# The small matmuls of the attention and of y between the big matmuls of the next slot, not in blocks between slots

## The chip, the cores and the metric

One NeuronCore of a Trainium2 chip runs the whole kernel. The metric is the time of one execution on the device, in microseconds (us). The engines are named PE (TensorE, matmuls), PEld (its weight loads), DVE (VectorE), ACT (ScalarE), POOL (GpSimd) and SP (SyncE, which issues DMAs).

## The reference: what is computed

One layer of a decoder trunk on x of 512 x 2048, float32. All of it is written with matmuls whose float32 operands are split exactly into a high and a low part (hi, lo), so that one product takes three matmuls.

```python
h = x @ w_in + b_in            # q,k,v,z of three branches, forget logits, three merge gates
o_fox  = fox_attention(...)    # 8 heads, causal, bias from cumulative log-sigmoid of the forget logits
o_swa  = swa_attention(...)    # 8 q heads / 2 kv heads, window 128, sinks, ALiBi
o_moba = moba_attention(...)   # 8 heads, blocks of 256, top-3 past blocks and the own one, ALiBi
br_i = (merge_heads(o_i) * silu(z_i)) @ w_branch_i
y = sum_i sigmoid(gate_i) * br_i
out = layer_norm(2 ** 0.25 * x + y @ w_out)
```

## The kernel before

The program is unrolled by Python; tiles carry their dependencies, and each engine runs its instructions in the order in which they are written. First come the V projection and the merge gates (up to about 530 us), which the change leaves alone. Then the main loop (line 1040) runs over a stream of weight tiles `ids`, one tile of 128x512 per **slot**: "h" slots (four per projected tile of 128 columns, `proj_step`), "v" slots (the V of moba, `mv_step`, 16 of them), "b" slots (branch products, four per group of 512 columns and branch, `branch_step`) and "o" slots (output product, `out_step`). An h, b or o slot issues 12 matmuls of 512 columns, a v slot 24 of 256 columns. These are the big matmuls.

At each slot i the loop first issues the high part of the weights of slot i + 2 on ACT (`prepare`), then the slot's big matmuls, then the tasks that were put down for slot i, sorted by an order number. The low part of those weights (`lower`, on DVE) is a task of order 2; when it is done it lets SP load raw weights further ahead. Three buffers hold the split weights.

The attention is put down as tasks by `plan_pair`. A head has four units (one for each 128 queries). A unit that begins at slot s does: scores at s, order 8 (`unit_scores`, two matmuls of 128 to 512 columns); maximum on DVE at s + 1, order 0 (`unit_max`) and exponential on ACT, order 5; reciprocal on DVE and scaling on POOL at s + 2, order 1; transposes at s + 3, order 8 (`unit_turn`, one to four of 128x128); their high part on ACT and low part on DVE at s + 4, orders 1 and 6. A head's values (`head_values`, 8 matmuls of 128 to 512 columns) are at order 8 six slots after its last unit began; its low half on ACT and its sum on DVE come one slot later, orders 2 and 7. Units begin 1.5 slots apart (fox, three pairs of heads of moba) or 1 slot apart (swa, the last pair). Order 8 comes last in a slot, so these matmuls stand in a block between the big matmuls of two slots. Projected tiles are evacuated one and two slots after their end, at orders 2 and 3 (`q_upper`, `k_lower` and so on).

In the b slots a group's fourth slot is followed by `branch_evac` (order 9: four products with the gates on DVE, and for two of three branches four sums). After the third branch of a block of 512 columns, `turn_y` runs at order 8 two and three slots later, twice each: four transposes and a split of the result, high part on ACT, low part on DVE.

PSUM has two sets of tiles: "acc" with three (projections, one of a branch's four, transposes of y) and "att" with five (scores, transposes, values, three of a branch's four).

Of the kernel before, what the change touches and what calls it, by code (L numbers as in the profile page):

```python
# [13 lines left out]
P = 128  # L14
# [73 lines left out]
def hybrid_kernel(ctx: ExitStack, tc: tile.TileContext, a: dict, out: bass.AP):  # L88
    nc = tc.nc
# [9 lines left out]
    ident = stage.tile([P, P], F32, name="ident", bufs=1)  # L99
# [9 lines left out]
    def acc_tile(name):  # L109
        return psum.tile([P, S], F32, tag="acc", name=name, bufs=3)  # L110

    def att_tile(name):
        return psum.tile([P, S], F32, tag="att", name=name, bufs=5)

    def split(raw, hi, lo):
        nc.scalar.activation(hi, raw, AF.Copy)  # L116
        nc.vector.tensor_sub(lo, raw, hi.bitcast(F32))  # L117
# [7 lines left out]
    def at(i, order, f, *args):  # L125
        tasks.setdefault(i, []).append((order, len(tasks.get(i, ())), f, args))
# [6 lines left out]
    def prepare(i):  # L133

        if i >= len(ids) or i in parts:
            return None
        load(i // 2)
        raw = raws[i // 2][:, (i % 2) * S:(i % 2 + 1) * S]
        if i in held:
            hi, lo = held[i]  # L140
        else:
            hi = stage.tile([P, S], F32R, tag="hi", name="hi")
            lo = stage.tile([P, S], F32R, tag="lo", name="lo")
        parts[i] = (hi, lo)
        nc.scalar.activation(hi, raw, AF.Copy)  # L145

        def lower():
            nc.vector.tensor_sub(lo, raw, hi.bitcast(F32))  # L148
            for d in range(1, raw_bufs):
                load(i // 2 + d)  # L150

        return lower
# [324 lines left out]
    for n in range(items):  # L477
        sc, m = divmod(n, 56)
# [85 lines left out]
        nc.sync.dma_start(a["scratch"], rows[:NH])  # L564


    halves = (slice(0, HD), slice(HD, P))

    def q_upper(acc, t, res):
# [56 lines left out]
    def unit_scores(kind, h, i, env, u):  # L626
        if i == 0:
            env["pth"] = work.tile([P, 13, P], F32R, tag="pth", name="pth")
            env["ptl"] = work.tile([P, 13, P], F32R, tag="ptl", name="ptl")
        u["k0"] = max(i - 1, 0) if kind == "swa" else 0  # L630
        u["n"] = (i + 1 - u["k0"]) * P
        ks = slice(u["k0"] * P, (i + 1) * P)
        qs, (kh, kl) = env["q"][env["e"]], env["k"][env["g"]]
        qi = qs[:, i * P:(i + 1) * P]
        s = u["s"] = att_tile("s")[:, :u["n"]]
        nc.tensor.matmul(s, qi, kh[:, ks], start=True, stop=False)
        nc.tensor.matmul(s, qi, kl[:, ks], start=False, stop=True)

    def unit_max(kind, h, i, env, u):
        n = u["n"]  # L640
# [32 lines left out]
        nc.gpsimd.tensor_scalar(lt, lt, st[:, 3:4], 1.0, op0=ALU.mult, op1=ALU.mult)  # L673

    def unit_turn(kind, h, i, env, u):
        pt = u["pt"] = att_tile("pt").rearrange("p (b c) -> p b c", c=P)
        for b in range(u["n"] // P):
            nc.tensor.transpose(pt[:, b], u["lt"][:, b * P:(b + 1) * P], ident)

    def cells(kind, i, u):  # L680
        nb = u["n"] // P
# [7 lines left out]
        nc.vector.tensor_sub(env["ptl"][:, c], u["pt"][:, :u["n"] // P], env["pth"][:, c].bitcast(F32))  # L689

    def head_values(kind, h, env):
        o = env["o"] = att_tile("o")
        for kb in range(4):
            q1 = min(kb + 2, 4) if kind == "swa" else 4
            cell = 2 * kb if kind == "swa" else 4 * kb
            for m, pp in enumerate((env["pth"], env["ptl"])):
                nc.tensor.matmul(o[:, kb * P:q1 * P], env["v"]()[:, kb, env["vh"]], pp[:, cell:cell + q1 - kb],
                                 start=(kb == 0 and m == 0), stop=(kb == 3 and m == 1), skip_group_check=True)

    def head_low(kind, h, env):  # L700
        mine = halves[env["e"]]
# [48 lines left out]
    def proj_step(i):  # L750
        _, t, c = ids[i]
        if c == 0:
            accs[t] = acc_tile(f"h{t}")
        hi, lo = parts.pop(i)
        for j in range(4):
            k, cc = 4 * c + j, slice(j * P, (j + 1) * P)
            nc.tensor.matmul(accs[t], hi[:, cc], xh[:, k], start=(k == 0), stop=False)  # L757
            nc.tensor.matmul(accs[t], hi[:, cc], xl[:, k], start=False, stop=False)  # L758
            nc.tensor.matmul(accs[t], lo[:, cc], xh[:, k], start=False, stop=(k == KD - 1))  # L759
        if c == 3:  # L760
            for d, order, f, res in ends[t]:
                at(i + d, order, f, accs[t], t, res)
# [3 lines left out]
    def mv_step(i):  # L766
        _, hf, g = ids[i]
        if g == 0:
            mv_acc[hf] = [acc_tile(f"mv{hf}{j}") for j in range(2)]
        hi, lo = parts.pop(i)  # L770
        for j in range(2):
            k, cc = 2 * g + j, slice(j * 256, (j + 1) * 256)
            for st in range(4):
                o = mv_acc[hf][st // 2][:, (st % 2) * 256:(st % 2 + 1) * 256]
                lx = slice(st * P, (st + 1) * P)
                nc.tensor.matmul(o, xh[:, k, lx], hi[:, cc], start=(k == 0 and st % 2 == 0), stop=False,
                                 skip_group_check=True)
                nc.tensor.matmul(o, xl[:, k, lx], hi[:, cc], start=False, stop=False, skip_group_check=True)
                nc.tensor.matmul(o, xh[:, k, lx], lo[:, cc], start=False, stop=(k == KD - 1),
                                 skip_group_check=True)  # L780
        if g == 6:
            mv_acc["b", hf] = work.tile([P, S], F32, tag="T", name="vbm")[:, :256]
            nc.sync.dma_start(mv_acc["b", hf], a["bm"][hf:hf + 1].to_broadcast([P, 256]))
        if g == 7:
            for st in range(4):
                at(i + st // 2, 9, mv_evac, hf, st)
# [22 lines left out]
    t = 0  # L809
    last_att = 0  # L810
    for p in range(4):
        q, k, z = [], [], []
# [28 lines left out]
    for p in range(4):  # L841
        q, k, z = [], [], []
# [12 lines left out]
    sigs, ys = {}, {}  # L855
# [18 lines left out]
    def branch_step(i):  # L874
        _, g, kt = ids[i]
        b = g % 3
        if kt == 0:
            for st in range(4):
                bracc[g, st] = (acc_tile if st == 3 else att_tile)("br")
        hi, lo = parts.pop(i)  # L880
        oh, ol = box["ozh"], box["ozl"]
        for st in range(4):
            ss = slice(st * P, (st + 1) * P)
            for n, (w, o) in enumerate([(hi, oh), (hi, ol), (lo, oh)]):
                nc.tensor.matmul(bracc[g, st], o[:, 4 * b + kt, ss], w, start=(kt == 0 and n == 0),  # L885
                                 stop=(kt == 3 and n == 2))
        if kt == 3:
            at(i, 9, branch_evac, g)
            if b == 2:
                for dt in range(4):  # L890
                    at(i + 2 + dt // 2, 8, turn_y, g // 3, dt)
# [14 lines left out]
    yb = {}  # L906

    def turn_y(dblk, dt):
        if not yb:
            yb["h"] = keep.tile([P, KD, S], F32R, tag="bigh", name="yh")  # L910
            yb["l"] = keep.tile([P, KD, S], F32R, tag="bigl", name="yl")
        yt = acc_tile("yt")
        for st in range(4):
            nc.tensor.transpose(yt[:, st * P:(st + 1) * P], ys[dblk, st][:, dt * P:(dt + 1) * P], ident)
        k = 4 * dblk + dt
        split(yt, yb["h"][:, k], yb["l"][:, k])

    zr, stats = [], []

# [18 lines left out]
    def out_mm(st, k, hi, lo, half=None):  # L938

        sl = slice(st * P, (st + 1) * P)  # L940
        o = oacc[st]
        if half is not None:
            cs = slice(half * 256, (half + 1) * 256)
            o, hi, lo = oacc[3 + half][:, :256], hi[:, cs], lo[:, cs]
        nc.tensor.matmul(o, yb["h"][:, k, sl], hi, start=(k == 0), stop=False)  # L945
        nc.tensor.matmul(o, yb["l"][:, k, sl], hi, start=False, stop=False)  # L946
        nc.tensor.matmul(o, yb["h"][:, k, sl], lo, start=False, stop=(k == KD - 1))  # L947
# [6 lines left out]
    def out_step(i):  # L954
        _, ec, k = ids[i]
        if k == 0:
            for st in range(4):
                oacc[st] = (acc_tile if st == 3 else att_tile)("o")
            if ec == 3:
                oacc[4] = acc_tile("o")  # L960
        if ec == 3 and k >= 4:
            return
        hi, lo = parts.pop(i)
        for st in range(3 if ec == 3 else 4):
            out_mm(st, k, hi, lo)
        if ec == 3:
            out_mm(3, k, hi, lo, 0)
            out_mm(3, k, hi, lo, 1)
        if k == KD - 1:
            for st in range(4):  # L970
                at(i, 9, residual, ec, st, oacc[st])
# [68 lines left out]
    for i in range(len(ids)):  # L1040
        assert i in parts
        lower = prepare(i + 2)
        if lower:
            at(i, 2, lower)
        step[ids[i][0]](i)
        for _, _, f, args in sorted(tasks.pop(i, ()), key=lambda x: x[:2]):
            f(*args)
    first = where["o", 3] + 4
# [83 lines left out]
```

## Time and profile before

| | us |
|---|---|
| runs | 1342.1, 1343.46, 1650.02 |
| median of the runs | 1343.46 |
| the profiled execution | 1342.68 |
| its span, which the trace covers | 1341.0 |
| PE busy in the span | 1323.1 |
| DVE / ACT / POOL busy | 906.3 / 647.6 / 177.2 |

The granted clock of PE is at its full level over all but the first and last of the 40 slices of the page. A matmul's row begins when it is taken up and its end is modelled, so rows of matmuls overlap; prices on PE are read from starts, over a stretch that begins and ends among big matmuls.

### The profile page before, as it was taken

How to read it: one execution, taken by the hardware profiler on the slowest of the kernel's cores; microseconds unless marked ns; L12 is line 12 of the kernel's file. 1: busy time of each engine (PE TensorE's matmuls, PEld its weight loads, DVE VectorE, ACT ScalarE, POOL GpSimd, SP SyncE). 2: the span in 40 equal slices, each digit the busy share in tenths (PEclk: the TensorE clock that was granted, in tenths of full speed). 3: DMA queues.
4: the chain of work that ended last, by engine and by line, in shares of the span. 5: the costliest groups of instructions: out<-in, count | busy, mean ns of one | idle time of the engine just before them, and what ended most of it. 6: DMA issues, size and time to landing. Idle time of an engine off the chain costs nothing.

```text
span 1341.0 us, 18413 instructions
## 1 busy us (share of the span) xinstructions
PE 1323.1 (99%) x6435; PEld 1115.8 (83%) x6435; DVE 906.3 (68%) x1629; ACT 647.6 (48%) x1195; POOL 177.2 (13%) x249
## 2 busy tenths in 40 slices
PE   8999999999999999999999999999999999999996
PEld 8888888888888888888889998888888888888885
DVE  7888888888888887566665656555646666532356
ACT  5445645455554645556564556565654222222231
POOL 4700000000000000111222333121220000000005
PEclk9999999999999999999999999999999999999998
DMA  7634427080633514432323232322225555453323
GB/s 246 223 142 163 159 65 266 9 300 29 214 116 112 211 32 145 152 96 80 110 71 99 64 86 77 94 67 92 71 81 183 185 188 189 158 218 94 94 95 126
DMA packets 57804, 174.43 MB, mean 130 GB/s; under 512 B 6552, under 2 KB 8088, under 8 KB 56944
## 3 DMA queue, kind: packets, MB, share of 16 engines
q1 hardware_dynamic: 46672, 145.87, 33.4%
q0 software_dynamic: 2976, 13.48, 2.9%
q10 hardware_dynamic: 8064, 13.91, 2.8%
q8 instruction: 50, 0.82, 0.2%
q14 instruction: 42, 0.34, 0.1%
HBM read 155.12 MB, written 18.12 MB: 129 GB/s over the span
## 4 chain that ended last, share of the span: by engine, by line
PE 97%; DVE 1%; issue 0%; DMA 0%; SPq 0%; ACT 0%; DVEq 0%; ACTq 0%
PE br L885 10%; PE h L757 9%; PE h L759 9%; PE h L758 9%; PE beta L325 5%; PE beta L323 5%; PE beta L324 5%; PE o L947 4%; PE o L945 4%; PE o L946 4%; PE gamma L325 3%; PE alpha L325 3%; PE gamma L323 3%; PE gamma L324 3%; PE alpha L323 3%; PE alpha L324 3%
## 5 line engine op out<-in xcount | busy, mean ns | idle before, releaser
L145 ACT ACTIVATE hi<-raw 128x512 fp32r<-128x512 f32 x248 | 156.3, 631 | 321.9 <-PE o L946 97.5
L148 DVE TENSOR_TENSOR lo<-raw,hi 128x512 fp32r<-128x512 f32 x248 | 174.1, 706 | 153.1 <-ACT hi L145 128.5
L757 PE MATMUL h<-xh,hi 128*128 128x512 f32 x528 | 208.0, 394 | 0.0
L759 PE MATMUL h<-xh,lo 128*128 128x512 f32 x528 | 206.6, 391 | 0.0
L758 PE MATMUL h<-xl,hi 128*128 128x512 f32 x528 | 206.1, 390 | 0.0
L759 PEld LDWEIGHTS h<-xh,lo 128*128 128x128 f32 x528 | 99.1, 188 | 21.8 <-DVE lo L148 0.3
L758 PEld LDWEIGHTS h<-xl,hi 128*128 128x128 f32 x528 | 99.3, 188 | 18.6
L757 PEld LDWEIGHTS h<-xh,hi 128*128 128x128 f32 x528 | 99.2, 188 | 18.5
L673 POOL TENSOR_SCALAR lt<-lt,st 128x128 f32<-128x128 f32 (+2 forms) x96 | 70.7, 737 | 289.5 <-DVE st L672 287.6
L116 ACT ACTIVATE ghi<-rawb 128x512 fp32r<-128x512 f32 x96 | 60.7, 633 | 69.8 <-DVE glo L117 47.3
L116 ACT ACTIVATE ghi<-rawd 128x512 fp32r<-128x512 f32 x96 | 60.7, 633 | 69.8 <-DVE glo L117 52.1
L116 ACT ACTIVATE ghi<-rawa 128x512 fp32r<-128x512 f32 x96 | 60.6, 633 | 52.0 <-PE alpha L324 17.3
L117 DVE TENSOR_TENSOR glo<-rawd,ghi 128x512 fp32r<-128x512 f32 x96 | 66.4, 691 | 24.0 <-ACT ghi L116 21.8
L945 PE MATMUL o<-hi,yh 128*128 128x512 f32 (+1 forms) x212 | 81.8, 386 | 0.0
L946 PE MATMUL o<-hi,yl 128*128 128x512 f32 (+1 forms) x212 | 81.7, 385 | 0.0
L947 PE MATMUL o<-lo,yh 128*128 128x512 f32 (+1 forms) x212 | 81.7, 385 | 0.0
L117 DVE TENSOR_TENSOR glo<-rawb,ghi 128x512 fp32r<-128x512 f32 x96 | 66.3, 690 | 18.8 <-ACT ghi L116 17.7
L325 PE MATMUL alpha<-glo,xh 128*128 128x512 f32 x192 | 75.2, 392 | 0.4 <-DVE glo L117 0.4
L885 PE MATMUL br<-hi,ozh 128*128 128x512 f32 x192 | 75.3, 392 | 0.0
L885 PE MATMUL br<-lo,ozh 128*128 128x512 f32 x192 | 74.9, 390 | 0.0
L325 PE MATMUL beta<-glo,sh 128*128 128x512 f32 x192 | 74.8, 390 | 0.0
L323 PE MATMUL alpha<-ghi,xh 128*128 128x512 f32 x192 | 74.8, 389 | 0.0
(231 smaller groups left out, 3108.5 us busy)
## 6 DMA issues: line engine op xcount, KB each, us to landing
raw<-in_ws SPq DMA_DIRECT2D x130, 512.0 KB, 3.5
rawc<-in_wa SPq DMA_DIRECT2D x24, 512.0 KB, 5.7
rawd<-in_wa SPq DMA_DIRECT2D x24, 512.0 KB, 5.5
sig<-gate_tiles SPq DMA_DIRECT2D x48, 256.0 KB, 3.9
rawb<-in_wa SPq DMA_DIRECT2D x20, 512.0 KB, 3.6
rawa<-in_wa SPq DMA_DIRECT2D x20, 512.0 KB, 4.8
rawv<-in_wv SPq DMA_DIRECT2D x15, 324.0 KB, 4.3
xraw<-in_xT SPq DMA_DIRECT2D x16, 256.0 KB, 4.8
```

The source lines that it names most:

```text
L116: nc.scalar.activation(hi, raw, AF.Copy)
L145: nc.scalar.activation(hi, raw, AF.Copy)
L148: nc.vector.tensor_sub(lo, raw, hi.bitcast(F32))
L323: nc.tensor.matmul(o, sth[:, us], hi, start=first, stop=False, skip_group_check=True)
L324: nc.tensor.matmul(o, stl[:, us], hi, start=False, stop=False, skip_group_check=True)
L325: nc.tensor.matmul(o, sth[:, us], lo, start=False, stop=last, skip_group_check=True)
L757: nc.tensor.matmul(accs[t], hi[:, cc], xh[:, k], start=(k == 0), stop=False)
L758: nc.tensor.matmul(accs[t], hi[:, cc], xl[:, k], start=False, stop=False)
L759: nc.tensor.matmul(accs[t], lo[:, cc], xh[:, k], start=False, stop=(k == KD - 1))
L885: nc.tensor.matmul(bracc[g, st], o[:, 4 * b + kt, ss], w, start=(kt == 0 and n == 0), stop=(kt == 3 and n == 2))
L945: nc.tensor.matmul(o, yb["h"][:, k, sl], hi, start=(k == 0), stop=False)
L946: nc.tensor.matmul(o, yb["l"][:, k, sl], hi, start=False, stop=False)
```

## The change

A list `small` is set up. The score matmuls, the transposes of the attention, the value matmuls, the transposes of y and the split of y behind them are no longer issued at their order in the slot, but put on that list as closures, in the order in which they were issued. In the next slot `begin_small(12)` sets how many closures one `tick()` takes from it (one up to twelve entries, two up to 24), and after each big matmul a `tick()` follows (two after three matmuls in a v slot, three after three in an o slot). What is left after the slot's big matmuls is issued then, ahead of the slot's other tasks. The PSUM tile of a score, transpose or value is taken when its first closure runs. Nothing else moves: the tasks that read the results keep their slots and orders.

```diff
+    small, rate = [], [1]
+
+    def begin_small(n):
+        rate[0] = max(1, -(-len(small) // n))
+
+    def tick(n=None):
+        for _ in range(rate[0] if n is None else n):
+            if small:
+                small.pop(0)()
...
-        s = u["s"] = att_tile("s")[:, :u["n"]]
-        nc.tensor.matmul(s, qi, kh[:, ks], start=True, stop=False)
-        nc.tensor.matmul(s, qi, kl[:, ks], start=False, stop=True)
+
+        def upper():
+            u["s"] = att_tile("s")[:, :u["n"]]
+            nc.tensor.matmul(u["s"], qi, kh[:, ks], start=True, stop=False)
+
+        small.append(upper)
+        small.append(lambda: nc.tensor.matmul(u["s"], qi, kl[:, ks], start=False, stop=True))
...
-        pt = u["pt"] = att_tile("pt").rearrange("p (b c) -> p b c", c=P)
+        def turn(b):
+            if b == 0:
+                u["pt"] = att_tile("pt").rearrange("p (b c) -> p b c", c=P)
+            nc.tensor.transpose(u["pt"][:, b], u["lt"][:, b * P:(b + 1) * P], ident)
+
         for b in range(u["n"] // P):
-            nc.tensor.transpose(pt[:, b], u["lt"][:, b * P:(b + 1) * P], ident)
+            small.append(lambda b=b: turn(b))
...
+        def value(kb, m):
+            if kb == 0 and m == 0:
+                env["o"] = att_tile("o")
             q1 = min(kb + 2, 4) if kind == "swa" else 4
             cell = 2 * kb if kind == "swa" else 4 * kb
...
+        for kb in range(4):
+            for m in range(2):
+                small.append(lambda kb=kb, m=m: value(kb, m))
...
             nc.tensor.matmul(accs[t], hi[:, cc], xh[:, k], start=(k == 0), stop=False)
+            tick()
             nc.tensor.matmul(accs[t], hi[:, cc], xl[:, k], start=False, stop=False)
+            tick()
             nc.tensor.matmul(accs[t], lo[:, cc], xh[:, k], start=False, stop=(k == KD - 1))
+            tick()
...
                 nc.tensor.matmul(o, xh[:, k, lx], lo[:, cc], start=False, stop=(k == KD - 1),
                                  skip_group_check=True)
+                tick()
+                tick()
...
                 nc.tensor.matmul(bracc[g, st], o[:, 4 * b + kt, ss], w, start=(kt == 0 and n == 0),
                                  stop=(kt == 3 and n == 2))
+                tick()
...
-        yt = acc_tile("yt")
+        box_y, k = {}, 4 * dblk + dt
+
+        def turn(st):
+            if st == 0:
+                box_y["t"] = acc_tile("yt")
+            nc.tensor.transpose(box_y["t"][:, st * P:(st + 1) * P], ys[dblk, st][:, dt * P:(dt + 1) * P], ident)
+
         for st in range(4):
-            nc.tensor.transpose(yt[:, st * P:(st + 1) * P], ys[dblk, st][:, dt * P:(dt + 1) * P], ident)
-        k = 4 * dblk + dt
-        split(yt, yb["h"][:, k], yb["l"][:, k])
+            small.append(lambda st=st: turn(st))
+        small.append(lambda: split(box_y["t"], yb["h"][:, k], yb["l"][:, k]))
...
             out_mm(st, k, hi, lo)
+            tick()
+            tick()
+            tick()
...
+        begin_small(12)
         step[ids[i][0]](i)
+        tick(len(small))
```

## Rows read from the trace of the kernel before

**Rows 1.** The page, part 1: engine, busy us (share of the span), instructions.

```profile
PE 1323.1 (99%) x6435; PEld 1115.8 (83%) x6435; DVE 906.3 (68%) x1629; ACT 647.6 (48%) x1195; POOL 177.2 (13%) x249
```

**Rows 2.** Waits of PE, whole span: us in total, times, longest us.

```profile
PE vc L251 <- DVE lo L117: 2.4, 3, 1.5
...
PE gamma L325 <- DVE glo L117: 0.4, 1, 0.4
```

**Rows 3.** Groups by line and form, PE: count, busy us, mean ns.

```profile
L678 PE MATMUL pt<-ident,lt 128*128 128x128 f32 x216 | 39.6, 274 | 0.0
...
L914 PE MATMUL yt<-ident,y 128*128 128x128 f32 x64 | 8.3, 272 | 0.0
...
L636 PE MATMUL s<-kh,qs 128*128 128x128 f32 x24 | 7.2, 299 | 0.0
```

**Rows 4.** Timeline of PE, big matmuls in a row: start us, us.

```profile
676.64 0.39 PE L757 MATMUL h<-xh,hi 128*128 128x512 f32 x1
...
681.18 0.39 PE L759 MATMUL h<-xh,lo 128*128 128x512 f32 x1
```

**Rows 5.** Timeline of PE, eight transposes of y between big matmuls.

```profile
1054.90 0.39 PE L885 MATMUL br<-lo,ozh 128*128 128x512 f32 x1
1055.13 1.03 PE L914 MATMUL yt<-ident,y 128*128 128x128 f32 x8
...
1056.46 0.40 PE L885 MATMUL br<-lo,ozh 128*128 128x512 f32 x1
```

**Rows 6.** Timeline of PE, two transposes alone between big matmuls.

```profile
831.75 0.39 PE L759 MATMUL h<-xh,lo 128*128 128x512 f32 x1
831.98 0.38 PE L678 MATMUL pt<-ident,lt 128*128 128x128 f32 x2
...
832.90 0.40 PE L757 MATMUL h<-xh,hi 128*128 128x512 f32 x1
```

**Rows 7.** Timeline of PE, the running sum's four matmuls between big ones.

```profile
545.77 0.39 PE L759 MATMUL h<-xh,lo 128*128 128x512 f32 x1
545.99 0.74 PE L560 MATMUL csum<-tri,pair 128*128 128x512 f32 x4
...
547.33 0.40 PE L757 MATMUL h<-xh,hi 128*128 128x512 f32 x1
```

**Rows 8.** Timeline of PEld, weight loads around two scores of 128 columns.

```profile
844.34 0.19 PEld L636 LDWEIGHTS s<-kh,qs 128*128 128x128 f32 x1
844.57 0.19 PEld L637 LDWEIGHTS s<-kl,qs 128*128 128x128 f32 x1
844.68 0.19 PEld L757 LDWEIGHTS h<-xh,hi 128*128 128x128 f32 x1
844.79 0.19 PEld L758 LDWEIGHTS h<-xl,hi 128*128 128x128 f32 x1
```

**Rows 9.** Timelines of PE and DVE, a block with values and after it.

```profile
674.03 0.39 PE L697 MATMUL o<-pth,vfox 128*128 128x512 f32 x1
...
675.95 0.40 PE L757 MATMUL h<-xh,hi 128*128 128x512 f32 x1
...
676.33 0.55 DVE L652 CUSTOM_DVE_ANT_0 lt<-s,row 128x384 f32<-128x384 f32 x1
...
677.28 0.67 DVE L148 TENSOR_TENSOR lo<-raw,hi 128x512 fp32r<-128x512 f32 x1
```

**Rows 10.** Tiles yt and br, 1050 to 1066: ns min/median/max of one.

```profile
L116 ACT ACTIVATE yh<-yt x4: 594/596/598, 1055.8 to 1059.9; 128x512 fp32r<-128x512 f32 x4
L117 DVE TENSOR_TENSOR yl<-yt,yh x4: 680/686/692, 1056.4 to 1060.6; 128x512 fp32r<-128x512 f32 x4
...
L899 DVE TENSOR_TENSOR y<-br,sig x4: 679/679/681, 1061.8 to 1063.6; 128x512 f32<-128x512 f32 x4
```

**Rows 11.** Windows, the part with attention: busy us by engine, clock, DMA.

```profile
530.00:1017.00 487.00, 487.00 (x2573) 416.62 (x2572) 281.95 (x721) 279.43 (x577) 109.77 (x169) 1.00 0.30 93
```

More of the change, by code (lines that the diff above doesn't have):

```diff
@@ L691, in head_values @@
     def head_values(kind, h, env):
-        o = env["o"] = att_tile("o")
-        for kb in range(4):
+        pth, ptl = env["pth"], env["ptl"]
+        def value(kb, m):
+            if kb == 0 and m == 0:
+                env["o"] = att_tile("o")
             q1 = min(kb + 2, 4) if kind == "swa" else 4
             cell = 2 * kb if kind == "swa" else 4 * kb
-            for m, pp in enumerate((env["pth"], env["ptl"])):
-                nc.tensor.matmul(o[:, kb * P:q1 * P], env["v"]()[:, kb, env["vh"]], pp[:, cell:cell + q1 - kb],
-                                 start=(kb == 0 and m == 0), stop=(kb == 3 and m == 1), skip_group_check=True)
+            nc.tensor.matmul(env["o"][:, kb * P:q1 * P], env["v"]()[:, kb, env["vh"]],
+                             (pth, ptl)[m][:, cell:cell + q1 - kb], start=(kb == 0 and m == 0),
+                             stop=(kb == 3 and m == 1), skip_group_check=True)
+        for kb in range(4):
+            for m in range(2):
+                small.append(lambda kb=kb, m=m: value(kb, m))
     def head_low(kind, h, env):
```

## The prediction

> **What bounds the kernel now.** I read the page first, then TensorE's waits, then TensorE's order of time where small matmuls stand between big ones, then VectorE's and ScalarE's rows at the two places where the change makes somebody wait. The page gives TensorE 99% of the span [rows 1]. Its waits add up to 6.7 us and all of them are before the attention: its five kinds belong to the V projection, the warm-up and the gates [rows 2] (first and last of the five). So from the projections of the attention on, TensorE never stands still, and what the change can win there is not a wait. It can only be the price that a small matmul has on TensorE.
>
> How many are there? 216 transposes of the attention and 64 of y [rows 3]; 24 heads with 4 units of two score matmuls, 192; 24 heads with 8 value matmuls, 192. In all 664. Today they stand in about 111 blocks: 8 of y, the others one at the end of each slot that has any (counted from the planner's slots).
>
> The prices follow from start times. Twenty big matmuls in a row take 681.18 - 676.64 = 4.54 us, 0.227 each [rows 4]. Eight transposes: from the last big one before them at 1054.90 to the third big one after, 1056.46, are 1.56 us; three big ones are 0.68, so 0.88 is left, 0.110 per transpose [rows 5]. Two transposes alone: 832.90 - 831.75 = 1.15 us with four big ones (0.91) leaves 0.24, so 0.12 each [rows 6]. A block thus costs 0.11 per transpose and 0.02 once, for leaving it. A single 128-column matmul of the other kind is seen once, as the last of the four of the running sum: 547.33 - 545.77 = 1.56 us less four big ones leaves 0.65; its 1,280 columns at 0.227 per 512 are 0.567, so the last one, with 0.057 for its columns, cost 0.057 + 0.083 = 0.14 [rows 7].
>
> Why 0.11 and not 0.057? The weight loads show it. Around a pair of 128-column scores the loads start at 844.34 (under the big one), 844.57, 844.68 and 844.79 [rows 8]. The first small load is hidden by the big matmul. The next two follow 0.11 apart: a load begins when the matmul before it gets going, so only one is ahead, and 128 columns are too short to cover 0.11 of load.
>
> **The change, part by part.** *Removed:* nothing; the same 664 instructions and loads are issued. *Moved on TensorE:* each small one now follows a big one and is followed by a big one (in pairs in the moba V slots, in threes in the output slots). The load of the small one was hidden for the first of a block and is now hidden for all. But the load of the big one behind it has only the small one to hide under, so 0.11 is paid there instead. Per small one I expect no gain, and a bit of the 0.02 on leaving: 664 less 111 blocks, less some 50 that still go in pairs or threes, is 500 new exits. Bounds from the nearest rows: nothing (the 0.02 may lie in how the next few big ones settle, which now overlap), and 0.14 - 0.11 = 0.03 (the single one of the running sum), that is 0 to 15 us. I take half of the 0.02, because transposes are the largest group and the two alone are their nearest row: 500 x 0.01 = 5.0 us. A gain is not excluded by this row alone; it is the first rival.
>
> The Trainium skill, page "TensorE: Matmul & The Clock Gate", section "Back-to-back issue gap", gives about 81 ns per matmul of 128 columns in a stream of loads and matmuls. No such row is here: the trace has 0.11. By the page's figure the 280 transposes would cost 8 us less, an estimate from that page alone.
>
> *Moved for the consumers:* scores, transposes and values, done at a slot's start until now, are done part of the way into it. Lists are mostly of 3 to 6, so they end by mid slot. The worst is a slot with values: 8 values, 2 transposes, 2 scores make 12, one per big one, with the scores last. Such a list costs 675.95 - 674.03 = 1.92 us [rows 9], so the slot lasts 12 x 0.227 + 1.92 = 4.64 us, and the last score ends about 0.4 behind that (a 512-column matmul's row lasts 0.39 [rows 4]). On VectorE the maximum (unit_max) stands ahead of the low half (lower) of the weights for the slot after next. From the maximum's start at 676.33 to the end of the low half behind it at 677.28 + 0.67 are 1.62 us [rows 9]. So these weights are ready 0.4 + 1.62 = 2.0 us into the next slot. They are needed at the third matmul of the slot after: 2.72 + 0.45 = 3.2 us, as the next slot has no list. Spare: about 1.1 us. The exponential behind the maximum on ScalarE delays only the next slot's high half, with a slot to spare. Cost: nothing, hidden by weights prepared two slots ahead; if that cover is gone, it is the second rival. Score and transpose tiles are given back within their own slot, so five suffice. No DMA and nothing on POOL is moved; the loads on SP wait for a low half that is up to 2 us later, and have about three pairs of slots in hand.
>
> *y:* the two transposes-and-splits of a slot now run in the next slot, so the second pair falls into the slot that ends the next branch product, and its splits go ahead of lower and of the evacuation (branch_evac) on VectorE. From that slot's start: nine big and eight transposes, 2.04 + 0.9, then the row of a transpose 0.27 [rows 3], the high part 0.60, the low part 0.69, the first product 0.68 [rows 10] and ahead of it lower with 0.67 [rows 9]: 5.85 us. Of att's five tiles three hold this branch, two are free, so the next branch's third tile waits for that first product. TensorE wants it after 12 big, 8 transposes and 6 big: 4.09 + 0.9 = 5.0 us. That is a new wait of 0.85, three times (the last y falls among the output slots): 2.5 us. Ends: 0 if the tiles are handed out otherwise, and 5 if the split is later by another row.
>
> **Sum**, against the profiled execution's own 1342.68 us (span 1341.0, 1.7 outside; the median of the runs shown, 1343.46, lies 0.8 above): + 5.0 + 2.5 = 1350.2, say 1350. With the bounds alone 1343 to 1363.
>
> **The rivals.** *The loads are hidden after all* (faster). If the chip can have two loads ahead when a big matmul gives it 0.227 for two of 0.11, each 128-column instruction falls from 0.11 to 0.057. These are 280 transposes, 48 scores [rows 3] and 48 values (two per head): 376 x 0.053 = 20 us less, with y's wait + 2.5: 1325. Against it: the running sum's last, with 512, 384 and 256 columns ahead of it, paid 0.14 [rows 7]. For it: only that one is seen. The Trainium skill's page "TensorE: Matmul & The Clock Gate", section "Step-by-step: what each phase is for", says that TensorE's window pulls weight loads ahead of running matmuls into a background buffer; the trace agrees for one load [rows 8], and that page by itself would allow this rival. Chance 0.08.
>
> *Late scores become TensorE's wait* (slower). Place: the third big matmul, two slots after each of the 24 slots with values. It decides once VectorE is over 1.1 us further behind there than worked out (a sigmoid's table load ahead of the exponential, or a key's low halves in the queue). For it: VectorE has long queues after some values. Against: it is busy 282 of 487 us in this part [rows 11]. Price, with 1 us each, 24 us on top of 7.5: about 1374; half of them 1362. Chance 0.14, about half of it over 2%.
>
> *Nothing moves*: exits settle for nothing and y's wait does not come, 1343. It is the low end of my own case, which has 0.75 in all; 0.03 are left for what I have not seen.
>
> **How the numbers follow.** Likeliest: 1350, own range 1340 to 1363. For eight in ten I go below to 1336, leaving out the first rival, and above to 1366, leaving out the dearer half of the second. A difference under 2% (27 us) counts as none here, about what a measurement of this kernel can tell. Faster by that would need 1316: not even the first rival has it, 0.02. Slower, over 1370: the dear half of the second rival, 0.07. Within: 0.91.
>
> **What would show it.** Right: TensorE's rows show transposes one by one, each with about 0.12 until the big one behind it runs, that big one's load starting when the small one gets going; no waits in the attention; three waits of some 0.9 us on y <- br in the branch products. Wrong: small ones at 0.06 (first rival), or waits of TensorE on VectorE's low halves (second). What would break the forecast most is an exit price above 0.03, which no row here excludes for alternation over a whole slot.

## The result

The changed kernel takes 1350.78 us (median of four runs, 1350.35 to 1351.37) against 1343.33 for the kernel before: a ratio of 1.0058, 95% interval 1.0046 to 1.0069. It is 0.6% slower, clear of the noise and far below 2%. One of the four runs of the kernel before took 1650.02 us; the ratio goes by the others. 1350 was forecast. The profiled execution has a span of 1348.8 us, 7.8 more than before.

The page of the changed kernel, part 1, and then three of its seven waits of PE (us in total, times, longest us):

```profile
PE 1328.4 (98%) x6435; PEld 1111.6 (82%) x6435; DVE 902.8 (67%) x1629; ACT 645.0 (48%) x1195; POOL 184.3 (14%) x249
```

```profile
PE vc L251 <- DVE lo L117: 2.4, 3, 1.5
...
PE br L916 <- DVE y L931: 1.6, 3, 0.5
...
PE h L787 <- DVE lo L148: 0.9, 1, 0.9
...
```

The first answers to [rows 1]: the same 6435 matmuls and loads, 5.3 us more busy time. The second answers to [rows 2]: two waits are new, on the first product of the next branch (three times, lines L916 and L931) and on a low half of the weights (once, L787 and L148). The granted clock is at its full level as before (0.997 over the span in both).

Where are the 7.8 us? The first matmuls of the projections, the branch products and the output product cut the time in parts. Timelines of PE, first before, then after:

```profile
529.65 0.39 PE L757 MATMUL h<-xh,hi 128*128 128x512 f32 x1
...
1016.95 0.39 PE L885 MATMUL br<-hi,ozh 128*128 128x512 f32 x1
...
1153.06 0.39 PE L945 MATMUL o<-hi,yh 128*128 128x512 f32 x1
```

```profile
529.42 0.40 PE L783 MATMUL h<-xh,hi 128*128 128x512 f32 x1
...
1021.82 0.39 PE L916 MATMUL br<-hi,ozh 128*128 128x512 f32 x1
...
1160.77 0.39 PE L982 MATMUL o<-hi,yh 128*128 128x512 f32 x1
```

The projections with the attention take 492.40 in place of 487.30 us, 5.1 more; the branch products 138.95 in place of 136.11, 2.8 more; all the rest is the same to 0.2. In the branch products the small ones now stand like this (PE, then PEld, start and length):

```profile
1063.94 0.48 PE L916 MATMUL br<-hi,ozl 128*128 128x512 f32 x1
1064.26 0.27 PE L949 MATMUL yt<-ident,y 128*128 128x128 f32 x1
...
1064.61 0.27 PE L949 MATMUL yt<-ident,y 128*128 128x128 f32 x1
1064.63 0.48 PE L916 MATMUL br<-hi,ozh 128*128 128x512 f32 x1
```

```profile
1064.26 0.19 PEld L916 LDWEIGHTS br<-lo,ozh 128*128 128x128 f32 x1
1064.40 0.14 PEld L949 LDWEIGHTS yt<-ident,y 128*128 128x128 f32 x1
1064.61 0.19 PEld L916 LDWEIGHTS br<-hi,ozh 128*128 128x128 f32 x1
1064.74 0.14 PEld L949 LDWEIGHTS yt<-ident,y 128*128 128x128 f32 x1
```

Two big matmuls, each with a transpose, take 0.69 us (1064.63 - 1063.94), 0.345 for one pair. Less 0.227 that leaves 0.118 for the transpose, against 0.110 in a block [rows 5]. The loads say why there is no gain. The load of the transpose starts 0.14 behind that of the big matmul and is done under it. But the load of the next big matmul starts at 1064.61, exactly when the transpose is taken up, and 0.13 to 0.14 pass before another follows. The cost has moved from the small one's load to the big one's.

The wait on y's splits: DVE's and PE's timelines at the end of a branch product.

```profile
1067.49 0.69 DVE L117 TENSOR_TENSOR yl<-yt,yh 128x512 fp32r<-128x512 f32 x1 [0.91 <-ACT yh L116]
1068.10 0.68 DVE L148 TENSOR_TENSOR lo<-raw,hi 128x512 fp32r<-128x512 f32 x1
1068.70 2.48 DVE L931 TENSOR_TENSOR y<-br,sig 128x512 f32<-128x512 f32 x4
...
1068.51 0.40 PE L916 MATMUL br<-lo,ozh 128*128 128x512 f32 x1
1069.44 0.50 PE L916 MATMUL br<-hi,ozh 128*128 128x512 f32 x1 [0.53 <-DVE y L931]
1069.78 0.40 PE L916 MATMUL br<-hi,ozl 128*128 128x512 f32 x1
```

The low part of y (1067.49) and the low half of the weights (1068.10) stand ahead of the first product (1068.70), and PE takes up its third group 0.93 behind the matmul before, 0.70 late, and the one after that 0.34 later, 0.11 late. That is 0.81 in all, three times 2.4 us. (The 0.53 in brackets counts only from the modelled end of the matmul before.)

The wait on a low half, where the projection of swa's keys is evacuated right behind a slot with values: ACT, DVE, PE.

```profile
699.32 0.38 ACT L704 ACTIVATE pth<-pt 128x256 fp32r<-128x256 f32 x1 [3.32 <-PE pt L694]
...
700.34 2.77 ACT L596 ACTIVATE kh<-h,bT 64x512 fp32r<-64x512 f32 x4
703.14 0.72 ACT L682 ACTIVATE lt<-lt,st 128x512 f32<-128x512 f32 x1
...
703.99 0.16 DVE L687 RECIPROCAL st<-st 128x1 f32<-128x1 f32 x1 [0.96 <-ACT lt L682]
704.07 3.02 DVE L603 SCALAR_TENSOR_TENSOR kl<-h,bT,kh 64x512 fp32r<-64x512 f32 x4
707.12 0.69 DVE L148 TENSOR_TENSOR lo<-raw,hi 128x512 fp32r<-128x512 f32 x1
...
706.67 0.27 PE L694 MATMUL pt<-ident,lt 128*128 128x128 f32 x1
707.87 0.50 PE L787 MATMUL h<-xh,lo 128*128 128x512 f32 x1 [0.93 <-DVE lo L148]
708.21 0.27 PE L694 MATMUL pt<-ident,lt 128*128 128x128 f32 x1
```

The lateness comes by way of ACT. It has waited for the transposes (699.32), which now end late in the slot. The four high parts of the keys (2.77 us) stand behind that, an exponential behind them (703.14), its reciprocal on DVE (703.99), then four low parts of the keys (3.02 us), and only then the low half of the weights at 707.12. PE's next matmul begins 1.20 behind the transpose before it, where 0.03 is usual, and the next pair is 0.03 late too: 1.2 us.

A third and smaller kind, not foreseen: POOL multiplies a head's result (L736) ahead of scaling the rows that are to be transposed.

```profile
601.46 2.33 POOL L736 TENSOR_TENSOR ot<-otmp,ot 64x512 f32<-64x512 f32 x1 [0.55 <-DVE st L687]
603.77 1.12 POOL L688 TENSOR_SCALAR lt<-lt,st 128x512 f32<-128x512 f32 x1
...
604.59 0.39 PE L783 MATMUL h<-xh,hi 128*128 128x512 f32 x1
604.95 0.33 PE L694 MATMUL pt<-ident,lt 128*128 128x128 f32 x1
```

The transpose starts 0.36 behind the big one in place of 0.23, just after the scaling has ended (603.77 + 1.12). This happens three times (604.6, 645.1, 685.7), 0.44 us together.

### The profile page after: what moved, and what is told of

The parts are those of the page before. It is cut to its first block, busy times and chain, and to the rows that moved or that the text cites. A ratio compares the mean times of both kernels' runs of the same rounds, so it can differ in the third digit from the quotient of the medians.

```text
span 1348.8 us, 18386 instructions
## 1 busy us (share of the span) xinstructions
PE 1328.4 (98%) x6435; PEld 1111.6 (82%) x6435; DVE 902.8 (67%) x1629; ACT 645.0 (48%) x1195; POOL 184.3 (14%) x249
## 4 chain that ended last, share of the span: by engine, by line
PE 96%; DVE 2%; ACT 0%; issue 0%; DMA 0%; SPq 0%; DVEq 0%; ACTq 0%
PE br L916 9%; PE h L787 9%; PE h L785 9%; PE h L783 9%; PE beta L325 5%; PE beta L323 5%; PE beta L324 5%; PE o L983 4%; PE o L982 4%; PE o L984 4%; PE alpha L325 3%; PE gamma L325 3%; PE gamma L323 3%; PE gamma L324 3%; PE alpha L323 3%; PE alpha L324 3%
## 5 line engine op out<-in xcount | busy, mean ns | idle before, releaser
L148 DVE TENSOR_TENSOR lo<-raw,hi 128x512 fp32r<-128x512 f32 x248 | 172.5, 701 | 126.3 <-ACT hi L145 103.0
L785 PE MATMUL h<-xl,hi 128*128 128x512 f32 x528 | 217.5, 412 | 0.0
L787 PE MATMUL h<-xh,lo 128*128 128x512 f32 x528 | 213.2, 404 | 0.9 <-DVE lo L148 0.9
L783 PE MATMUL h<-xh,hi 128*128 128x512 f32 x528 | 211.3, 400 | 0.0
L787 PEld LDWEIGHTS h<-xh,lo 128*128 128x128 f32 x528 | 99.2, 188 | 24.1 <-DVE lo L148 1.5
L688 POOL TENSOR_SCALAR lt<-lt,st 128x128 f32<-128x128 f32 (+2 forms) x96 | 74.5, 776 | 297.7 <-DVE st L687 291.0
L682 ACT ACTIVATE lt<-lt,st 128x128 f32<-128x128 f32 (+3 forms) x96 | 51.6, 537 | 66.5 <-DVE st L687 30.5
L916 PE MATMUL br<-hi,ozh 128*128 128x512 f32 x192 | 76.7, 400 | 1.6 <-DVE y L931 1.6
L916 PE MATMUL br<-hi,ozl 128*128 128x512 f32 x192 | 76.4, 398 | 0.0
L916 PE MATMUL br<-lo,ozh 128*128 128x512 f32 x192 | 75.9, 395 | 0.0
```

## The experiments

The question: is the loss the price of standing alone on PE (an exit, as the prediction calls it), or the lateness that the move brings to the other engines? And is the price of a small matmul really the load of the one behind it?

**y alone, and the attention alone.** In the first the attention's closures are run at once, at their old place; in the second y's are.

```diff
+    def put(f):
+        f()
...
-        small.append(upper)
+        put(upper)
...
-            small.append(lambda b=b: turn(b))
+            put(lambda b=b: turn(b))
```

> Only the transposes and splits of y go between the big matmuls; scores, transposes and values of the attention stay in their blocks. Theory (exits of about 0.01 us for each small matmul that stands alone, plus three waits for the first product of the next branch): the branch part is longer by the 2.8 us that it has in the changed kernel, of them 2.1 waits and 0.7 exits, so 1346.1. Rival (the attention's delay is what costs, y is free): 1343.3.

> Only the attention's small matmuls go between the big ones; y stays in blocks. Theory: 3.6 us of exits, one wait of 1.1 for a low half and three small ones of 0.14 on a scaled row, together 5.1, so 1348.4; and with y's 2.8 the two parts add up to the changed kernel's 7.4 to 7.9. Rival (the two parts disturb each other, as delays on VectorE pile up): the sum of the two parts is short of the whole by 2 us or more.

Measured: y alone 1346.31 us, ratio 1.0023 (1.0014 to 1.0031). The attention alone 1349.29, ratio 1.0041 (1.0029 to 1.0054). The two excesses add up to 0.64%, the whole has 0.58%, within the intervals: the parts don't disturb each other. By the first matmuls of the parts, as above, y alone lengthens the branch products to 138.95 and leaves the projections at 487.32; the attention alone lengthens the projections to 492.38 and leaves the branch products at 136.13. These are the two excesses of the changed kernel to 0.02 us. That the profiled execution of the attention alone (1350.06 us) lies above the expected 1348.4 comes from ahead of the change: its projections begin at 531.93, those of the changed kernel at 529.42.

**The waits taken away.** The low half goes ahead of all other tasks of its slot, and in branch slots two small ones follow each big one.

```diff
-            at(i, 2, lower)
-        begin_small(12)
+            at(i, -1, lower)
+        begin_small(6 if ids[i][0] == "b" else 12)
```

> The changed kernel with its waits taken away: the low half of the weights goes ahead of every other task of its slot on VectorE, and in the branch slots two small matmuls follow each big one, so that y's splits end earlier. Theory (exits and waits are separate): the waits of 2.1 and 1.1 go and some of y's exits (0.3), 1347.3; 4 us over the kernel before stay, as these are no waits. Rival (all of the loss is waiting on other engines, some of it not shown as waits): 1343.5. A third (waits only move to the next late task): 1350.8.

Measured: 1346.74 us, ratio 1.0028 (1.0018 to 1.0038). The waits of PE in this kernel, all of them:

```profile
PE vc L251 <- DVE lo L117: 2.4, 3, 1.5
PE va L250 <- DVE xl L117: 2.0, 3, 1.4
PE warm L201 <- DVE warm L198: 1.5, 1, 1.5
PE va L249 <- ACT xh L116: 0.7, 2, 0.4
PE alpha L325 <- DVE glo L117: 0.4, 1, 0.4
```

Both new lines are gone, and so are the three transposes that POOL made late. The kernel is 4.0 us faster than the changed one, with 3.5 us over the kernel before left. The projections take 490.96 (3.7 over before), the branch products 136.41 (0.3 over). So about half of the loss was waiting and half is not, as the theory had it; the rivals (1343.5 and 1350.8) both fall. A little of the third rival is there: a transpose in a moba V slot is now late on its scaled row. It starts at 712.57, 0.36 behind the matmul before it where 0.12 is usual, and costs 0.3 us in all.

**One block, in the next slot.** The list is emptied behind the first big matmul.

```diff
-        begin_small(12)
+        begin_small(1)
```

> The whole list goes as one block behind the first big matmul of the next slot, in place of one per big matmul. Theory (each matmul that stands alone pays an exit, a block pays one): 1343.5, within 0.1% of the kernel before, since the results come only 0.23 us later than there. Rival (the move into the next slot costs, not the single standing): 1347 or more.

Measured: 1343.08 us, ratio 0.9999 (0.9990 to 1.0008). Projections 487.23, branch products 136.11. The move into the next slot costs nothing. What costs is that the small ones are spread: they stand alone, and the last of a list ends late.

**The price by itself.** To the kernel before, 528 small matmuls are added in 44 output slots, where no other small ones are, into a PSUM tile that nobody reads.

```diff
+    def extra(n):
+        for _ in range(n):
+            nc.tensor.transpose(dum[0][:, :P], ident, ident)
...
         nc.tensor.matmul(o, yb["h"][:, k, sl], hi, start=(k == 0), stop=False)
+        extra(more)
...
+            dum[0] = acc_tile("dum")
```

That is the run with one behind each big matmul; in the others `extra` is called with three behind every three big ones, or with twelve behind the slot's last. In the runs with 64, 256 and 512 columns the added line is a matmul of the big ones' kind:

```diff
-            nc.tensor.transpose(dum[0][:, :P], ident, ident)
+            nc.tensor.matmul(dum[0][:, :64], yb["h"][:, 0, :P], yb["h"][:, 0, :64], start=True, stop=True)
```

> The kernel before with 528 transposes more, of the identity into a PSUM tile that nobody reads: twelve as one block at the end of each of 44 output slots (the extra work is not part of the result). Theory: 0.109 each and 0.02 per block for leaving it, 58.4 us, so 1401.6.

> The same 528 transposes in the same slots, one behind each big matmul (extra work, not part of the result). Theory (the big matmul behind pays its weight load in place of the next transpose, and a bit for leaving): 0.1175 each as read in the branch slots of the changed kernel, 62.0 us, so 1405.2, that is 3.6 over the block. Rival (a load hidden under each big matmul is a load saved): 0.06 each, 1375.

> 528 matmuls with only 64 columns, of the same kind as the big ones, one behind each big matmul of the same slots, into a tile that nobody reads (extra work). Theory (what a small one costs is the weight load of the big one behind it, whatever its own columns): 0.11 to 0.12 each, 58 to 63 us, so 1401 to 1407. Rival (its columns set its price): 64 columns at 0.227 per 512 are 0.03, with a fixed 0.01 some 20 us, so 1363.

> The same with 256 columns, so four times the work of the run with 64 (extra work). Theory: 256 columns take 0.114, as long as the load that they hide, and pay 0.12 with what leaving costs: 63 us, 1406, so about as much as 64 columns. Rival (the load of the big one comes on top of the columns): 0.22 each, 1459; or by columns against 64: four times.

> The same 528 transposes as in the block and the single run, in threes behind every three big matmuls (extra work). Theory (the load of each costs 0.109, and the big matmuls behind a group run a little over 0.227 until they settle, which a new group cuts short): 176 groups at 3 x 0.109 + 0.02 = 61.1 us, 1404.3, the same as single (60.7) and twelve (60.4) within 0.1%. Rival (a fixed price for each group that is left, 0.05 as from the blocks of twelve): 66 us, 1409.

> The matmuls with 64 columns as twelve in a block at the slot's end (extra work). Theory (weight loads one after the other set the price in a block too, 0.109 each whatever the columns): 57.6 us and 0.05 per block, 60 us, 1403.2, close to 64 columns standing alone (61.5). Rival (a block of short ones runs by its columns, since loads are ahead there): 0.06 or less each, 1375.

> 528 matmuls of 512 columns, as long as the big ones, one behind each big matmul (extra work). Theory (a matmul long enough to hide the next load costs its columns and nothing for standing alone): 0.227 each, 119.9 us, 1463.1. Rival (standing alone costs 0.013 even so, as with 256 columns): 126.7 us, 1470.

The price of one is read from the high products of the output stage, first and last start of the line. The rows are those of the kernel before, then the block, the single ones, 64, 256 and 512 columns alone:

```profile
L945 PE MATMUL o<-hi,yh x212: 277/389/476, 1153.1 to 1296.2; 128*128 128x512 f32 x102, 128*128 128x256 f32 x4
```

```profile
L950 PE MATMUL o<-hi,yh x212: 277/397/481, 1153.9 to 1357.1; 128*128 128x512 f32 x102, 128*128 128x256 f32 x4
```

```profile
L950 PE MATMUL o<-hi,yh x212: 277/477/484, 1153.4 to 1357.5; 128*128 128x512 f32 x102, 128*128 128x256 f32 x4
```

```profile
L950 PE MATMUL o<-hi,yh x212: 277/476/477, 1153.5 to 1357.6; 128*128 128x512 f32 x102, 128*128 128x256 f32 x4
```

```profile
L950 PE MATMUL o<-hi,yh x212: 277/398/476, 1155.1 to 1365.1; 128*128 128x512 f32 x102, 128*128 128x256 f32 x4
```

```profile
L950 PE MATMUL o<-hi,yh x212: 277/389/476, 1156.0 to 1418.8; 128*128 128x512 f32 x102, 128*128 128x256 f32 x4
```

143.1 us have become 203.2, 204.1, 204.1, 210.0 and 262.8; in threes it is 203.0, and with 64 columns in a block 203.2. The times of whole runs also hold up to 3 us that lie ahead of this stage (it begins at 1153.1 before and at 1156.9 with 64 columns in a block), so the price goes by the rows. The increase divided by 528:

| added | time, us | ratio (interval) | by the rows, each, us |
|---|---|---|---|
| transposes, twelve in a block | 1403.61 | 1.0452 (1.0436 to 1.0467) | 0.114 |
| transposes, in threes | 1403.99 | 1.0453 (1.0435 to 1.0470) | 0.113 |
| transposes, alone | 1403.89 | 1.0455 (1.0439 to 1.0470) | 0.116 |
| 64 columns, twelve in a block | 1404.68 | 1.0458 (1.0442 to 1.0474) | 0.114 |
| 64 columns, alone | 1404.71 | 1.0460 (1.0444 to 1.0475) | 0.116 |
| 256 columns, alone | 1410.01 | 1.0496 (1.0478 to 1.0513) | 0.127 |
| 512 columns, alone | 1464.13 | 1.0902 (1.0885 to 1.0918) | 0.227 |

64 columns cost as much as a transpose of 128, and a quarter of the columns save only 0.011 of the 0.127 of 256. So below 256 columns the load sets the price, not the columns, and whoever stands in front of a big matmul pays for that one's load. PEld with 64 columns alone shows it: loads follow in pairs 0.11 apart, the second of a pair under the big matmul. (In no run does a short matmul go without a load of its own; that the floor is the load rests on these rows and [rows 8].)

```profile
1250.26 0.19 PEld L950 LDWEIGHTS o<-hi,yh 128*128 128x128 f32 x1
1250.37 0.19 PEld L940 LDWEIGHTS dum<-yh 128*128 128x128 f32 x1
1250.60 0.19 PEld L952 LDWEIGHTS o<-hi,yl 128*128 128x128 f32 x1
1250.71 0.19 PEld L940 LDWEIGHTS dum<-yh 128*128 128x128 f32 x1
```

The rivals that gave 1363 or 1375 for short ones alone, or 1375 in a block, fall by 29 us and more, and so does 1459 for 256 columns. 512 columns alone pay nothing beyond their own 0.227, as the theory expected. 256 columns cost 0.127 where 0.12 was expected, and 64 columns in a block came to 1404.68 where 1403.2 was.

The block missed its expectation: 1403.6 in place of 1401.6. So did the single ones: 1403.9 in place of 1405.2, 0.3 over the block and not 3.6. The 0.109 per transpose holds inside it (from the second on they start 0.108 to 0.110 apart), so the rest, 60.1 less 57.6, is 2.5 us for 44 blocks, 0.06 for each where 0.02 was put. PE behind a block shows the place:

```profile
1248.52 0.39 PE L952 MATMUL o<-hi,yl 128*128 128x512 f32 x1
...
1251.06 0.38 PE L940 MATMUL dum<-ident 128*128 128x128 f32 x2
```

Eleven big matmuls lie between 1248.52 and 1251.06: 0.231 each, where 0.227 is the rule [rows 4]. So behind this block the big ones run a few nanoseconds over their pace for a whole slot. Behind a block of 64 columns it is shorter: the last six big ones of such a slot (1248.57 to 1249.93 in that run) are back at 0.227. In threes or alone the next small one comes before they settle, so a fixed 0.05 per group (1409 for the threes) is wrong as well.

It is not short matmuls alone that do this. In the kernel before, PE's rows at the end of the gates and the start of the projections hold big matmuls only:

```profile
528.61 0.50 PE L325 MATMUL gamma<-glo,sh 128*128 128x512 f32 x1
528.95 0.40 PE L323 MATMUL gamma<-ghi,sh 128*128 128x512 f32 x1
...
531.26 0.39 PE L758 MATMUL h<-xl,hi 128*128 128x512 f32 x1
```

The first was taken up late, 0.40 behind the one before it; the ten from 528.95 to 531.26 take 0.231 each. In the rows read, then, the slower pace follows a break in the even row of big matmuls, a short one or a wait.

Hence over a stage like this standing alone costs next to nothing for transposes, 0.116 against 0.114, because each block of twelve pays for settling too. Against the 0.109 inside a block it is 0.007. For 256 columns it is somewhat more, 0.127 where the columns alone would take 0.114.

## Why the prediction was right

**No gain on PE.** Right, and shown: the load of the big one behind a small one is paid in place of the small one's own. The first rival (two loads ahead, 1325) is out by the runs with 64 columns. The Trainium skill's rule that was weighed there (loads are pulled ahead of running matmuls, page "TensorE: Matmul & The Clock Gate", section "Step-by-step: what each phase is for") agrees with these traces for one load ahead; nothing here shows a second. The 81 ns that the Trainium skill gives on the same page, section "Back-to-back issue gap", did not show: a transpose costs 0.109 to 0.118 in the rows read here.

**The exits.** 5.0 us were put (500 at 0.01, bounds 0 to 15). The attention's excess is 5.1, less waits of 1.2 and 0.44, so 3.5. y's 2.8 less 2.4 is 0.4. Together 3.9. The size was a little high. The picture was too simple in one point: the 0.02 isn't one price paid on leaving. A transpose that stands alone costs 0.007 over the 0.109 inside a block, and a few nanoseconds more fall on each of up to eleven big ones behind the last of a list, which the blocks paid as well. 500 times 0.007 is 3.5, near the 3.9 and the mended kernel's 4.0; this is an estimate, as scores and values were not measured alone.

**y's wait.** 0.85 was worked out, three times; 0.81 came, three times, at the place named (the first product of the next branch), and it went when the splits came earlier.

**Late scores.** The main case had no wait here, and 1.1 us to spare. That held for 23 of 24 heads' values. For the second head of the third pair of fox it did not: swa's keys are projected where a next pair's q would stand, so their evacuation falls right behind these values, which the working on one slot of the usual pair had not looked at. This is the second rival, with a trigger it named (a key's low halves in the queue), once, one slot later than the place it named, at 1.2 us, not at 24 us. It came by way of ScalarE, whose exponential the prediction gave a slot to spare. A sign of it stood in the kernel before: behind the first keys' low parts a big matmul (560.74) already has the next one 0.34 behind it in place of 0.227, so that "TensorE never stands still" was out by 0.1 us there.

The prediction also put POOL at nothing, as nothing on it is moved. Its order is the same, but its product of a head's result now comes just ahead of a scaling that PE needs: 0.44.

So the sum of 7.5 came out in part by luck: one term was 1.1 too high, and two that were put at nothing came to 1.6. 3.9 + 2.4 + 1.2 + 0.4 = 7.9, and the projections began 0.2 earlier.

**Open:** why big matmuls run at 0.231 behind a break, and how the 3.5 us of the attention divide among transposes, scores and values; only lone transposes, 64, 256 and 512 columns were measured by themselves. Summed from the starts of PE's rows, list by list, the 24 lists with values (279 small ones) took 1.3 us more than their blocks, the other 80 (325 small ones) 2.2 besides the waits: no kind holds it all.

## What to carry to other kernels

Where each matmul brings its own load and only one load is ahead, a short matmul costs the load of the next one, wherever it stands; so mixing short ones among long ones hid nothing here. Longer streams did hide the load (512 columns alone cost their own 0.227); fewer loads were not tried. Before spreading work that is not waited for, look at who reads its results in order on another engine: half of the loss here was queues behind a result that came later. Work such a delay through for the irregular slot (here the one projection without its partners), not for the usual one.

## What the hardware showed that was not expected

A matmul of 64 columns behind a long one costs 0.116 us, as much as a transpose of 128 columns and nearly as much as 256 columns (0.127). And behind a break, a block of transposes or a matmul taken up late, ten or eleven long ones took 0.231 in place of 0.227; behind a block of 64 columns the last six of a slot were back at 0.227.
